# Spreading the branch gates over the RWKV pairs, wider chain loads, and block-diagonal RWKV scores in a hybrid attention / RWKV-7 / PEER layer

## The chip, the cores and the metric

One core of a Trainium2 chip runs the whole layer as one program. The metric is device time in microseconds of that core, as a median of runs. Besides TensorE (PE; its weight loads are PEld), VectorE (DVE), ScalarE (ACT), GpSimd (POOL) and SyncE (SP), the core has 16 DMA engines. DMAs are issued from in-order queues, here those of SP, ACT and POOL.

## The reference

One layer of a diffusion backbone on 512 latent tokens with a prefix of 256 context tokens, model width 1024, all in fp32.

```python
zx = split(modulate(rmsnorm(x, norm1_g), mod_x[0], mod_x[1]) @ w_in, IN_SPLIT_IDX)   # and zc of the context
o_ax = diff_post(diff_attention(qx, k_all, v_all, lam), ...)        # 8 heads, 512 queries on 768 keys
_, y_x = wkv_scan(s_ctx, scan_x)                                    # RWKV-7, 16 heads of 64, two directions
o_bx = rwkv_post(from_scan(y_x), ...)
g_a, g_b = split(sigmoid(zx[4]), 2)                                 # branch gates: 2 x 1024 columns of w_in
x = x + mod_x[2] * ((g_a * (o_ax @ w_branch_a) + g_b * (o_bx @ w_branch_b)) @ w_out)
x = x + mod_x[5] * peer_ffn(modulate(rmsnorm(x, norm2_g), ...), ...)  # top 16 of 16384 experts, 8 heads

def step(s, inp):                                                   # one token of the RWKV scan
    w, kk, a, k, v, r = inp
    sa = einsum('dbhij,dbhj->dbhi', s, kk)
    s = s * w[..., None, :] - sa[..., :, None] * (kk * a)[..., None, :] + v[..., :, None] * k[..., None, :]
    return s, einsum('dbhij,dbhj->dbhi', s, r)
```

## The kernel before

A framework puts the instructions of each engine into one fixed order: it simulates the program, takes the earliest instruction of the program text that its simulation finds ready, and fills gaps with later ones. So what stands later in the text can run earlier, across the stages below. Tiles come from pools with a fixed number of buffers, and an instruction waits until its buffer is free.

A product of full precision is three passes (`mm3`): weights and activations are split into a high part (ACT, line 95, `w_hi`) and a low part (DVE, line 96, `w_lo`). One column tile of 128 with 512 tokens is 24 matmuls of 512 columns.

The stages in order of time:

- **Set-up** (to about 65 us): modulation, norm, `hidden`, which also writes the modulated hidden state to the scratch tensor `hD`.
- **RWKV pairs** (`rw_pairs`, about 65 to 545 us): eight pairs of heads. Pair p projects k, r and v of pair p+1 (`rw_proj`, `shifted`; PSUM pool `pps` of 4 banks), makes the decayed operands `At` and `kb` of both directions (`rw_operands`), the bonus and transposed values (`rw_values`), and the chunk scores (`rw_scores`). The scores are 64x64 matmuls: per group of 8 chunks and per direction 16 of them into one `pq` tile of two banks (pool of 2 tiles), head 0 on rows 0 to 63, head 1 on rows 64 to 127. ACT copies `tt` and `kt` out, DVE masks `bt`, and SP stores them to the DRAM tensors `readD`, `scoreD`, `KBD`, `tD`, in runs of 1 KB for the first three. `rw_inverse` inverts 128 32x32 triangles at a time on DVE, in pairs 2, 3, 4, 6, 7 and after the last. Pair 7, which has no next projection, runs the first 5 (`NG`) of 16 gate tiles instead (`filler`).
- **Attention projections** (about 545 to 765 us): q, k, v of four head pairs.
- **Chain** (`rwkv_chain`, about 765 to 1112 us): 24 chunks of 32 tokens, one after the other, in two groups g: `reads` (line 659), `solve` (669), `state` (681, 687), `outputs` (700), `collect`. `load(c + 1)` fetches a chunk: per head side `cb` from `readD` and `scoreD` (64 partitions each) and `KBt` in runs of 512 bytes, `sv` and `XTz`; 14 DMAs on SP's queue, into 2 buffers (3 for `sv`). Attention (`attention`) fills the gaps: the first 25 of its 32 (head, query block) combines use PSUM pool `psO`; the last 7 use `psR`, a pool opened after the chain's PSUM is free. Heads 1 to 7 load `qr`, `kr`, `va` on POOL's queue (`att_load`).
- **Attention's end and gates** (about 1112 to 1206 us): `rwkv_centre`, the 7 last combines, `attention_norm`, and `gates`: the hidden state is read back from `hD`, split again, and gate tiles 5 to 15 are projected.
- **Merge** (`merge`, about 1206 to 1345 us), and **PEER** (to the end): `peer_route`, `peer_gates`, and `block_acts` for blocks of 128 experts, whose PSUM tile `ps_a` has 2 banks (`pa`) that ACT's gelu (line 1121) frees.

Of the kernel before, what the change touches and what calls it, by code (L numbers as in the profile page):

```python
# [9 lines left out]
F32 = mybir.dt.float32  # L10
# [11 lines left out]
S = 512  # L22
# [8 lines left out]
class K:  # L31
# [68 lines left out]
    def consts(self):  # L100
# [25 lines left out]
        self.hD = dt("hD", [KT, 128, S])  # L126
# [16 lines left out]
    def consts_late(self):  # L143
# [11 lines left out]
        self.ka1 = cp.tile([128, 8], F32, name="ka1")  # L155
        nc.vector.tensor_scalar(self.ka_, self.ka_, 0.5, None, op0=OP.mult)
        nc.vector.tensor_scalar(self.ka1, self.ka_, -1.0, 1.0, op0=OP.mult, op1=OP.add)
# [62 lines left out]
    def hidden(self, xt, n, i, hi, lo, pool):  # L220

        nc = self.nc
        for kt in range(KT):
# [4 lines left out]
            if i == 0:  # L228
                nc.sync.dma_start(self.hD[kt], h)
# [95 lines left out]
    NG = 5  # L325

    def gate(self, n, hx, gp, pp, tag):
# [6 lines left out]
        g = gp.tile([128, S], F32, name="st_r", bufs=2)  # L334
        nc.scalar.activation(g, px, AF.Tanh, scale=0.5)
        nc.sync.dma_start(self.gateD[n], g)

    def gates(self, gp, pp):
        nc = self.nc
        self.wn = 128  # L340
        hx = [gp.tile([128, KT, S], F32R, name=f"gh{i}") for i in range(2)]
        for kt in range(KT):
            raw = gp.tile([128, S], F32, name="gr", bufs=2)
            nc.sync.dma_start(raw, self.hD[kt])
            nc.scalar.copy(hx[0][:, kt], raw)
            nc.vector.tensor_tensor(hx[1][:, kt], raw, hx[0][:, kt].bitcast(F32), op=OP.subtract)
        for n in range(self.NG, 16):
            self.gate(n, hx, gp, pp, "ps_gt")
# [6 lines left out]
    def rwkv_open(self, es):  # L355
# [10 lines left out]
        self.At = self.Ai[:, :3072].rearrange("p (c a d x) -> p c a d x", c=12, a=2, d=2)  # L366
        for j in range(2):
            h = slice(64 * j, 64 * j + 64)
            nc.vector.tensor_copy(self.Ai[h, 3072:], self.ident[h, h])
# [78 lines left out]
    def rw_proj(self, p, mids=()):  # L448
# [11 lines left out]
        for o in (0, H):  # L460
            ps = self.ps.tile([128, 512], F32, name="pp")
            nc.tensor.matmul(ps[:, :H], self.bones, kk[:, o:o + H], start=True, stop=True)
            rs = self.rsqrt(self.stage1, ps[:, :H], H, 1.0, 1e-12, tag="kk")
            nc.vector.scalar_tensor_tensor(kk[:, o:o + H], k[:, o:o + H], self.kk_[:, p:p + 1], rs,
# [3 lines left out]
    def rw_operands(self, p, sg, k, kk, r):  # L468
# [5 lines left out]
        for dr in range(2):  # L474
# [5 lines left out]
            nc.vector.tensor_scalar(w, w, 1.0, None, op0=OP.add)  # L480
            nc.vector.tensor_tensor_scan(L, self.smask, w, 0.0, op0=OP.mult, op1=OP.add)
# [5 lines left out]
            for tk, cs in parts:  # L487
                nc.vector.scalar_tensor_tensor(kb[:, cs, 32:64], ch(a)[:, cs], 1.0, ch(fl(kk[:, tk])),
                                               op0=OP.add, op1=OP.mult)
# [4 lines left out]

            kr = (lambda x: x[:, :, ::-1]) if dr else (lambda x: x)
            for tk, cs in parts:
                nc.vector.tensor_tensor(kr(kb[:, cs, 0:32]), ch(fl(k[:, tk])), ch(a)[:, cs], op=OP.mult)
            wc = ch(w)
            if dr == 0:
                k2 = kb.rearrange("p c (i t) -> p c i t", i=2)  # L500
                nc.vector.tensor_tensor(k2, k2, wc[:, :, None, :].to_broadcast([128, 24, 2, 32]), op=OP.mult)
            else:
                nc.vector.tensor_tensor(kb[:, :, 0:32], kb[:, :, 0:32], kr(wc), op=OP.mult)
                nc.vector.tensor_tensor(kb[:, :, 32:64], kb[:, :, 32:64], wc, op=OP.mult)
            KB.append(kb)
        for j in range(2):
            nc.sync.dma_start(self.readD[:, j, :, p].rearrange("c r a d x -> r c (a d x)"),
                              self.At[64 * j:64 * j + 64].rearrange("p c a d x -> p c (a d x)"))
# [84 lines left out]
    def rw_pairs(self, filler):  # L593
# [3 lines left out]
        for p in range(8):  # L597
# [7 lines left out]
            if p in (2, 3, 4, 6, 7):  # L605
                self.rw_inverse((2, 3, 4, 6, 7).index(p))
# [851 lines left out]
```

## Time and profile before

| | |
|---|---|
| median of 3 runs | 2692.36 us (2684.4 to 2698.49) |
| profiled execution | 2696.16 us, span 2693.7 us |
| PE busy | 2448.3 us (91% of the span) |
| PE weight loads | 2097.4 us (78%) |
| DVE busy | 1973.3 us (73%) |
| ACT busy | 1180.8 us (44%) |
| POOL busy | 384.9 us (14%) |
| chain that ended last | PE 62%, DVE 15%, DMA 12%, ACT 5%, issue 4% |

Busy shares are means over stages with different limits, and matmuls overlap: their shown duration is longer than the interval at which they follow each other.

### The profile page before, as it was taken

To read this page: it belongs to the slowest core of one execution; us is meant where nothing else is said; L and a number is where in the kernel's file an instruction comes from. 1 tells how busy PE (TensorE), PEld (TensorE's weight loads), DVE (VectorE), ACT (ScalarE), POOL (GpSimd) and SP (SyncE) were. 2 spreads that over 40 slices of the span, in tenths; PEclk is the share of its full clock that TensorE was granted. 3 is DMA by queue.
4 is the path that set the end of the run, shared out by engine and by line. 5 is a ranking of instruction groups with operands and counts; after the bars stand their busy time and mean duration, and the time that the engine had idled before them with its cause. 6 is when DMAs were issued, how large, how long until landed. Compare 5 with 4: busy or idle time off the path is not lost.

```text
span 2693.7 us, 47831 instructions
## 1 busy us (share of the span) xinstructions
PE 2448.3 (91%) x18877; PEld 2097.4 (78%) x18877; DVE 1973.3 (73%) x3661; ACT 1180.8 (44%) x2173; POOL 384.9 (14%) x322
## 2 busy tenths in 40 slices
PE   6888777799979878999989988999999999989898
PEld 3776666688968767787768887998889999867677
DVE  5778987773547556748469998886587888878894
ACT  4676555433346555645243343554233333323232
POOL 0000000000110000000000000003344444444440
PEclk8999988799989999999989999999999999999999
DMA  6376666767579877544432443678999999999993
GB/s 256 99 158 153 152 136 155 196 200 244 143 171 204 165 154 151 129 133 133 160 125 95 140 150 129 257 264 337 331 336 329 339 327 336 337 356 366 380 336 109
DMA packets 344912, 584.04 MB, mean 217 GB/s; under 512 B 85552, under 2 KB 238768, under 8 KB 337904
## 3 DMA queue, kind: packets, MB, share of 16 engines
q1 hardware_dynamic: 293744, 400.74, 50.7%
q0 software_dynamic: 39664, 146.16, 15.5%
q10 hardware_dynamic: 11280, 34.08, 3.8%
q8 instruction: 148, 2.42, 0.4%
q14 instruction: 76, 0.62, 0.1%
HBM read 473.03 MB, written 107.48 MB: 216 GB/s over the span
## 4 chain that ended last, share of the span: by engine, by line
PE 62%; DVE 15%; DMA 12%; ACT 5%; issue 4%; SPq 2%; POOL 0%; ACTq 0%; DVEq 0%; POOLq 0%
PE ps_v L1149 6%; PE ps_v L1151 6%; PE ps_v L1148 6%; PE ps_a L78 5%; PE ps_a L79 5%; PE ps_a L80 5%; PE pp L78 4%; PE pp L79 4%; PE pp L80 4%; DMA cb<-scoreD 3%; PE ps_br L80 2%; PE ps_br L79 2%; PE ps_br L78 2%; PE ps_s L681 1%; PE ps_o L814 1%
## 5 line engine op out<-in xcount | busy, mean ns | idle before, releaser
L78 PE MATMUL ps_a<-h,u_hi 128*128 128x384 f32 x1024 | 349.1, 341 | 19.7 <-ACT act L1121 17.7
L80 PE MATMUL ps_a<-h,u_lo 128*128 128x384 f32 x1024 | 348.7, 341 | 5.9 <-DVE u_lo L72 5.9
L79 PE MATMUL ps_a<-h,u_hi 128*128 128x384 f32 x1024 | 346.8, 339 | 0.0
L69 ACT CAST u_hi<-u_raw 128x1024 fp32r<-128x1024 f32 x128 | 134.4, 1051 | 305.3 <-PE ps_a L79 284.4
L1086 POOL DMA_INDIRECT gr<-in_peer_u,ei x128 | 164.0, 1281 | 705.7 <-PE ps_a L79 483.1
L72 DVE TENSOR_TENSOR u_lo<-u_raw,u_hi 128x1024 fp32r<-128x1024 f32 x128 | 156.1, 1220 | 111.8 <-ACT u_hi L69 110.4
L78 PEld LDWEIGHTS ps_a<-h,u_hi 128*128 128x128 f32 x1024 | 195.1, 190 | 25.6 <-ACT act L1121 21.0
L1086 POOL DMA_INDIRECT gr<-in_peer_v,ei x128 | 179.9, 1406 | 202.4 <-DVE ra L1104 182.8
L80 PEld LDWEIGHTS ps_a<-h,u_lo 128*128 128x128 f32 x1024 | 194.5, 190 | 9.1 <-DVE u_lo L72 8.1
L79 PEld LDWEIGHTS ps_a<-h,u_hi 128*128 128x128 f32 x1024 | 194.9, 190 | 2.3
L96 DVE TENSOR_TENSOR w_lo<-w_raw,w_hi 128x1024 fp32r<-128x1024 f32 (+1 forms) x93 | 124.9, 1343 | 86.9 <-ACT w_hi L95 83.4
L1093 DVE CUSTOM_DVE_ANT_0 gr<-gr,ht 128x1024 f32<-128x1024 f32 x128 | 153.8, 1219 | 13.9 <-DMA gr<-in_peer_u,ei 13.8
L1104 DVE SCALAR_TENSOR_TENSOR ra<-gr,wk,ra 128x1024 f32<-128x1024 f32 x127 | 162.7, 1281 | 1.2 <-DMA gr<-in_peer_v,ei 0.2
L552 PE MATMUL pq<-At,kb 64*64 64x128 f32 x1536 | 115.6, 300 | 46.4 <-DVE bt L559 36.3
L1149 PE MATMUL ps_v<-v_lo,pw_hi 128*128 128x512 f32 x420 | 143.6, 402 | 11.4 <-DVE v_lo L1139 11.4
L552 PEld LDWEIGHTS pq<-At,kb 64*64 64x64 f32 x1536 | 98.1, 149 | 71.1 <-issue 59.6
L95 ACT CAST w_hi<-w_raw 128x1024 fp32r<-128x1024 f32 (+1 forms) x93 | 106.9, 1149 | 97.9 <-PE ps_br L79 52.1
L1148 PE MATMUL ps_v<-v_hi,pw_hi 128*128 128x512 f32 x420 | 126.3, 398 | 13.0 <-ACT v_hi L1138 13.0
L1151 PE MATMUL ps_v<-v_hi,pw_lo 128*128 128x512 f32 x420 | 133.7, 400 | 0.0
L69 ACT CAST pw_hi<-actl 128x384 fp32r<-128x384 f32 x72 | 37.0, 514 | 217.1 <-PE ps_v L1149 217.1
L1148 PE MATMUL ps_v<-w_hi,pw_hi 128*128 128x512 f32 x348 | 128.4, 401 | 4.0 <-issue 4.0
L1149 PE MATMUL ps_v<-w_lo,pw_hi 128*128 128x512 f32 x348 | 131.9, 398 | 0.0
(377 smaller groups left out, 6373.4 us busy)
## 6 DMA issues: line engine op xcount, KB each, us to landing
u_raw<-in_uT SPq DMA_DIRECT2D x128, 512.0 KB, 4.7
v_raw<-in_peer_v SPq DMA_DIRECT2D x70, 512.0 KB, 8.0
w_raw<-in_peer_v SPq DMA_DIRECT2D x58, 512.0 KB, 6.5
wm<-in_w_mod SPq DMA_DIRECT2D x24, 1024.0 KB, 7.8
gD<-gstage SPq DMA_DIRECT2D x12, 2048.0 KB, 9.3
gg<-gD SPq DMA_DIRECT2D x16, 1536.0 KB, 11.9
actD<-act SPq DMA_DIRECT2D x18, 768.0 KB, 3.8
actl<-actD SPq DMA_DIRECT2D x9, 1536.0 KB, 11.7
```

Of the source, the lines that this page charges most:

```text
L69: nc.scalar.copy(hi, raw)
L72: (lo_eng or nc.vector).tensor_tensor(lo, raw, hi.bitcast(F32), op=OP.subtract)
L78: mm(ps, lh[0], rh[0], start=first, stop=False)
L79: mm(ps, lh[0], rh[1], start=False, stop=False)
L80: mm(ps, lh[1], rh[0], start=False, stop=last)
L552: nc.tensor.matmul(ps[i][h, c, :], KB[dr][h, g, :], at, start=True, stop=True)
L1086: nc.gpsimd.indirect_dma_start(out=r, out_offset=None, in_=self.A[name], in_offset=bass.IndirectOffsetOnAxis(ap=self.ei[:, k:k + 1], axis=0))
L1093: nc.vector.tensor_tensor_reduce(out=r, in0=r, in1=self.ht, scale=1.0, scalar=0.0, op0=OP.mult, op1=OP.add, accum_out=w[:, k:k + 1])
L1104: nc.vector.scalar_tensor_tensor(self.ra, r, w[:, k:k + 1], self.ra, op0=OP.mult, op1=OP.add)
L1148: mm(pc[t][d], w[0][:, ts], v[0][:, c[d]], start=first, stop=False)
L1149: mm(pc[t][d], w[0][:, ts], v[1][:, c[d]], start=False, stop=False)
L1151: mm(pc[t][d], w[1][:, ts], v[0][:, c[d]], start=False, stop=last)
```

## The change

Gate tiles 2p and 2p+1 are now computed inside RWKV pair p from the hidden state in SBUF; `gates`, `hD` and the filler are gone. The scores use block-diagonal 128x128 operands `kz` (both heads in one matmul, zeros elsewhere); the multiplication by the decay `w`, which was three wide DVE instructions on `kb`, now writes `kz` in 36 small ones per pair. One PSUM pool of 7 banks serves the whole front part. Scores and operands go to `cbD` and `KBD`, laid out by chunk and row: stored in runs of 512 bytes, read with one 4 KB run per partition, `cb` over 128 partitions. `sv` and `XTz` loads of the chain go to POOL's queue. The normalisation of kk starts on ACT and has one DVE instruction less per half; `a + 1` is an instruction of its own. In PEER's first phase `block_acts` alternates between two pools of 2 banks.

```diff
@@ scratch tensors
-        self.readD = dt("readD", [12, 2, 64, 8, 2, 2, 64])
-        self.scoreD = dt("scoreD", [12, 2, 64, 8, 2, 2, 64])
-        self.KBD = dt("KBD", [12, 2, 64, 8, 2, 2, 64])
+        self.cbD = dt("cbD", [24, 256, 8, 2, 64])
+        self.KBD = dt("KBD", [24, 128, 8, 2, 64])
...
-            if i == 0:
-                nc.sync.dma_start(self.hD[kt], h)
...
@@ rw_proj
-            rs = self.rsqrt(self.stage1, ps[:, :H], H, 1.0, 1e-12, tag="kk")
+            nc.scalar.activation(y, ps[:, :H], AF.Abs_reciprocal_sqrt, bias=self.tiny)
+            nc.scalar.activation(q, y, AF.Square, scale=math.sqrt(0.5))
+            nc.vector.scalar_tensor_tensor(q, ps[:, :H], 1e-12, q, op0=OP.add, op1=OP.mult)
+            nc.vector.scalar_tensor_tensor(y, q, 1.5, y, op0=OP.subtract, op1=OP.mult)
...
@@ rw_operands
+            nc.vector.tensor_scalar(a, a, 1.0, None, op0=OP.add)
...
-            if dr == 0:
-                k2 = kb.rearrange("p c (i t) -> p c i t", i=2)
-                nc.vector.tensor_tensor(k2, k2, wc[:, :, None, :].to_broadcast([128, 24, 2, 32]), op=OP.mult)
-            else:
-                nc.vector.tensor_tensor(kb[:, :, 0:32], kb[:, :, 0:32], kr(wc), op=OP.mult)
-                nc.vector.tensor_tensor(kb[:, :, 32:64], kb[:, :, 32:64], wc, op=OP.mult)
...
@@ rw_scores
+            for i in range(2):
+                c4, g4 = slice(4 * i, 4 * i + 4), slice(cg * 8 + 4 * i, cg * 8 + 4 * i + 4)
+                for dr in range(2):
+                    kz = self.kz[i][dr]
+                    for j in range(2):
+                        h = slice(64 * j, 64 * j + 64)
...
+                        if dr == 0:
+                            eng.tensor_tensor(zo, zi, w[0][h, g4, None, :].to_broadcast([64, 4, 2, 32]), op=OP.mult)
+                        else:
+                            eng.tensor_tensor(zo[:, :, 0, ::-1], zi[:, :, 0], w[1][h, g4], op=OP.mult)
+                            eng.tensor_tensor(zo[:, :, 1], zi[:, :, 1], w[1][h, g4], op=OP.mult)
+                    ps = self.ps.tile([128, 512], F32, name="pp").rearrange("p (c x) -> p c x", c=4)
                     for c in range(4):
...
-                            nc.tensor.matmul(ps[i][h, c, :], KB[dr][h, g, :], at, start=True, stop=True)
+                        nc.tensor.matmul(ps[:, c, :], kz[:, c, :], at, start=True, stop=True)
...
+            for dst, src in ((self.cbD[:, 64:192], bt), (self.KBD, kt)):
+                nc.sync.dma_start(dst[cg * 8:cg * 8 + 8, :, p].rearrange("c r d x -> r c (d x)"),
+                                  src.rearrange("p c d x -> p c (d x)"))
...
@@ rw_pairs
-            nx = self.rw_proj(p + 1, [lambda: ups((1, 0), (1, 1)), lambda: ups()]) if p < 7 else filler([lambda: ups((1, 0), (1, 1)), lambda: ups()])
+            mids = [lambda: ups((1, 0), (1, 1))]
+            nx = self.rw_proj(p + 1, mids) if p < 7 else mids[0]()
+            gate(2 * p)
             KB = self.rw_operands(p, sg, *st[:3])
...
+            gate(2 * p + 1)
             self.rw_values(p, st[0], st[2], st[3])
-            self.rw_scores(p, KB)
+            self.rw_scores(p, KB, sg)
...
@@ rwkv_chain, load(c)
-                ld(cb[j][h], rows(self.readD))
-                ld(cb[j][r], rows(self.scoreD))
-                ld(KBt[j][c % NL][r], rows(self.KBD))
+                ld(cb[j], self.cbD[c, 128 * j:128 * j + 128])
+                ld(KBt[j][c % NL][64 - 64 * j:128 - 64 * j], self.KBD[c, 64 * j:64 * j + 64])
                 for d, t in enumerate((32 * c, 32 * ((7 if c < 8 else 31) - c))):
-                    nc.sync.dma_start(sv[j][i][64 - 64 * j:96 - 64 * j, d], self.vTD[t:t + 32, j])
+                    nc.gpsimd.dma_start(sv[j][i][64 - 64 * j:96 - 64 * j, d], self.vTD[t:t + 32, j])
             for q in range(4):
-                nc.sync.dma_start(XTz[c % NL][32 * q:32 * q + 32, q], self.xD[q // 2, c, q % 2])
+                nc.gpsimd.dma_start(XTz[c % NL][32 * q:32 * q + 32, q], self.xD[q // 2, c, q % 2])
...
@@ block_acts, peer
-        ps = self.pa.tile([128, S], F32, name="ps_a")[:, :ND]
+        ps = (pa or self.pa).tile([128, S], F32, name="ps_a")[:, :ND]
...
-                    self.block_acts(g * AB + b, act[:, b, :])
+                    self.block_acts(g * AB + b, act[:, b, :], pa1 if b % 2 else None)
...
@@ front
-        pps = self.pool("pps", 4, space=PSUM)
-        self.ps = pps.__enter__()
         mps = self.pool("mps", 1, space=PSUM)
         self.mps = mps.__enter__()
+        pps = self.pool("pps", 7, space=PSUM)
...
@@ mixers
-                self.gates(gp, pp)
```

## Rows read from the trace of the kernel before

**Rows 1.** Windows by stage: PE, PEld, DVE, ACT, POOL busy (instructions); clock, DMA share, GB/s.

```profile
65.00:545.00 480.00, 389.75 (x2845) 316.80 (x2845) 378.79 (x766) 275.68 (x580) 4.44 (x8) 0.91 0.64 151
545.00:765.00 220.00, 214.24 (x1806) 198.81 (x1804) 112.61 (x189) 74.02 (x132) 10.38 (x10) 0.99 0.59 183
765.00:1112.00 347.00, 295.70 (x6242) 251.66 (x6243) 222.14 (x489) 192.26 (x436) 22.57 (x37) 0.93 0.86 170
1112.00:1206.00 94.00, 91.53 (x474) 75.12 (x472) 51.87 (x102) 53.84 (x105) 0.00 (x0) 1.00 0.42 133
1206.00:1345.00 139.00, 139.00 (x565) 106.16 (x565) 85.21 (x119) 54.88 (x75) 0.00 (x0) 1.00 0.48 151
1345.00:1850.00 505.00, 471.17 (x3002) 438.06 (x3001) 434.41 (x1065) 221.20 (x417) 6.46 (x7) 0.97 0.50 172
```

**Rows 2.** Waits in 765 to 1112 us: who, for whom, us, times, longest.

```profile
POOL va L766 <- PE ps_o L814: 170.1, 6, 49.5
...
PE ps_r L659 <- DMA cb<-scoreD: 16.3, 11, 2.9
...
PE ps_u L669 <- ACT rhs L662: 12.5, 3, 5.0
...
PE ps_r L659 <- DMA XTz<-xD: 6.6, 3, 3.5
```

**Rows 3.** DMA in 765 to 1112 us: a queue's packets, MB, share; issues with landing time.

```profile
q1 hardware_dynamic: 79399, 46.03, 69.8%
...
cb<-scoreD SPq DMA_DIRECT2D x44, 256.0 KB, 7.1
...
cb<-readD SPq DMA_DIRECT2D x43, 256.0 KB, 6.6
...
w_raw<-in_w_g SPq DMA_DIRECT2D x2, 512.0 KB, 4.6
```

**Rows 4.** Groups in 1112 to 1206 us: busy, mean ns, idle before them.

```profile
L96 DVE TENSOR_TENSOR w_lo<-w_raw,w_hi 128x1024 fp32r<-128x1024 f32 x13 | 15.9, 1222 | 21.7 <-ACT w_hi L95 18.6 <-ACT pdT L811 2.4 <-PE ps_gt L80 0.7
```

**Rows 5.** DVE groups in 65 to 545 us.

```profile
L559 DVE TENSOR_TENSOR bt<-pq,mask 128x256 f32<-128x256 f32 x96 | 40.3, 419 | 27.3 <-ACT kt L558 27.2
...
L501 DVE TENSOR_TENSOR kb<-kb,sgw 128x1536 f32<-128x1536 f32 x8 | 14.0, 1749 | 0.0
...
L480 DVE TENSOR_SCALAR sgw<-sgw 128x768 f32<-128x768 f32 x16 | 8.9, 554 | 2.0 <-ACT sgw L443 2.0
L53 DVE TENSOR_SCALAR kk_v<-pp 128x384 f32<-128x384 f32 x16 | 8.9, 553 | 6.0 <-PE pp L462 6.0
...
L504 DVE TENSOR_TENSOR kb<-kb,sgw 128x768 f32<-128x768 f32 x8 | 7.6, 950 | 0.0
...
L432 DVE TENSOR_TENSOR lul<-bo,luh 64x256 fp32r<-64x256 f32 x16 | 6.7, 419 | 7.0 <-ACT luh L429 6.8
...
L584 DVE TENSOR_TENSOR X<-X,Xt 128x135 f32<-128x135 f32 x10 | 2.9, 293 | 0.2
```

**Rows 6.** Timeline of DVE: start, duration; neighbours that overlap.

```profile
216.55 0.69 DVE L492 TENSOR_TENSOR At<-P,st_r 128x512 f32<-128x512 f32 x1
217.15 0.42 DVE L582 TENSOR_TENSOR Xt<-Tm,X 128x252 f32<-128x252 f32 x1
```

**Rows 7.** Chain that ended last: start, us, unbroken runs of matmuls.

```profile
496.59 1.92 PE pq L552 x28
...
1142.41 1.34 PE ps_o L814 x12
```

**Rows 8.** Windows: one 60 us stretch of the pairs, columns as in rows 1.

```profile
240.00:300.00 60.00, 47.25 (x402) 37.68 (x398) 51.30 (x116) 37.78 (x83) 1.11 (x2) 1.00 0.75 165
```

**Rows 9.** DMA in 65 to 545 us: SP's queue.

```profile
q1 hardware_dynamic: 95551, 54.95, 52.7%
```

**Rows 10.** Waits of PE in 1393 to 1850 us.

```profile
PE ps_a L78 <- ACT act L1121: 17.7, 11, 2.8
```

**Rows 11.** POOL's DMA issues by line: ns min/median/max.

```profile
L757 POOL DMA_DIRECT2D kr<-kTD x14: 587/597/602, 784.1 to 1021.8; - x14
```

More of the change, by code (lines that the diff above doesn't have):

```diff
@@ L333, in gate @@
             self.mm3(px, (w[0][:, kt], w[1][:, kt]), (hx[0][:, kt], hx[1][:, kt]), kt == 0, kt == KT - 1)
-        g = gp.tile([128, S], F32, name="st_r", bufs=2)
+        g = gp.tile([128, S], F32, name="st_g", bufs=1)
         nc.scalar.activation(g, px, AF.Tanh, scale=0.5)
         nc.sync.dma_start(self.gateD[n], g)
[L338 to L348, printed above, removed]
     def rwkv_open(self, es):
@@ L591, in rw_inverse, with rw_pairs @@
             o += n
-    def rw_pairs(self, filler):
+    def rw_pairs(self):
+        gate = lambda n: self.gate(n, self.hx, self.stage, self.ps, "pp")
         st = self.rw_proj(0)
@@ L1109, with block_acts @@
     AB = 4
-    def block_acts(self, n, out):
+    def block_acts(self, n, out, pa=None):
         nc = self.nc
@@ L1168, in peer @@
         with self.pool("rt1", 1, side="right") as b1, self.pool("pg", 4, space=PSUM) as self.pg, \
-                self.pool("ap", 2, side="left") as ap:
+                self.pool("ap", 2, side="left") as ap, self.pool("pa1", 2, space=PSUM) as pa1:
             self.row_tokens()
@@ L1287, in front @@
             self.hidden(ct, CT, 1, self.hc[0], self.hc[1], hp)
-        mps.__exit__(None, None, None)
-        with wps, self.pool("pqs", 2, space=PSUM) as self.pq, self.pool("stg", 2, side="right") as self.stage, self.pool("stg1", 1, side="right") as self.stage1:
+        with wps, self.pool("stg", 2, side="right") as self.stage, self.pool("stg1", 1, side="right") as self.stage1:
             inv = self.pool("inv", 1, side="left")
@@ L1296, in front @@
                 self.rw_lora(w0)
-                self.rw_pairs(lambda mids: [(f(), self.gate(n, self.hx, self.stage, self.ps, "pp"))
-                                            for n, f in enumerate(mids + [lambda: None] * (self.NG - 2))])
+                self.rw_pairs()
             inv.__exit__(None, None, None)
-        pps.__exit__(None, None, None)
-        mps = self.pool("mps", 1, space=PSUM)
-        self.mps = mps.__enter__()
-        pps = self.pool("pps", 7, space=PSUM)
-        self.ps = pps.__enter__()
         self.wn = 256
@@ L1348, in mixers @@
             self.wpool = self.wps.enter_context(self.pool("wp", 2, side="left"))
-            with self.pool("gt", 1, side="left") as gp, self.pool("rpp", 2, space=PSUM) as pp, \
+            with self.pool("rpp", 2, space=PSUM) as pp, \
                     self.pool("atr", 3, space=PSUM) as psR:
```

62 lines of the change are left out of this document (28 added, 34 removed).

## Prediction

> **What bounds the kernel now.** I read the windows by stage first. In the RWKV pairs (65 to 545 us) no engine is full: PE 389.75 and DVE 378.79 of 480 us, 81% and 79%, at a granted clock of 0.91. The attention projections are PE's (214 of 220). In the chain (347 us) PE is busy for 295.70 at 0.93, and the DMA engines for 0.86 of the time. The stretch behind the chain is PE's alone (91.53 of 94), and so is the merge (139 of 139): its 24 column tiles cost 139 / 24 = 5.8 us each [rows 1]. So work that moves from the stretch behind the chain into the pairs moves from a full PE to one with 90 us idle.
>
> The waits of the chain come next: PE stands 16.3 us for `cb<-scoreD` and 6.6 for `XTz`, and 12.5 at the start for ACT's `rhs`, which is queued there behind casts that await their own loads [rows 2]. The DMA view says why: SP's queue alone moves 46 MB in 79,399 packets, about 580 bytes each, and takes 69.8% of the engines' time; a half `cb` of 256 KB lands after 7.1 or 6.6 us, a whole weight tile of 512 KB after 4.6 [rows 3].
>
> **The change part by part.**
>
> *Gates leave the stretch behind the chain.* Eleven tiles of 5.8 us are 64 us of PE. What is left there: PE 91.5 - 64 = 27.5; on DVE 51.9 less eleven `w_lo` of 1.222 (13.4), 38 at most [rows 1, 4]. Left are the 7 last combines, which by their pool cannot start before the chain ends, and the norm. If they overlapped perfectly the stretch would be 38 us (-56). If the dependent steps of a combine kept their pace, it would shrink only a little; I set the weak end at -15. No engine is full there any more, but one combine is a line of PE, DVE, ACT, PE steps; I take 51 us, **-43**.
>
> *Gates enter the pairs: PE.* +64 us.
>
> *Scores, PE.* Before: 1536 instructions (each fp32 matmul shows as two); an unbroken run is 28 in 1.92 us, 69 ns each, 105 us. After: 384 whole-array matmuls, 768 instructions. The nearest are the 128x128 ones with 128 columns of attention: 12 in 1.34 us, 112 ns each, 86 us [rows 7]. So -19 us, and PE in the pairs comes to 390 + 64 - 19 = 435.
>
> The Trainium skill (TensorEngine Tiling (Array Packing), Theoretical Speedup) speaks against this part: a contraction of 64 or fewer rows gains up to 2x from splitting the array, and block-diagonal operands give that back. By that rule the scores would cost PE as much as before, and the sum would be 19 us of PE higher. The rows side with the change here, since the split instructions follow each other at 69 ns and not at half of 112.
>
> *Scores, DVE.* Per pair 12 instructions of 64x256 (419 ns, L432) and 24 of 64x128 (nearest 128x135, 293 ns, L584): 5.0 + 7.0 = 12.0 us. Away go one of 1749 (L501) and two of 950: 3.65. Net +8.4 by durations [rows 5]; neighbours on DVE overlap by some 0.09 us (216.55 + 0.69 against 217.15) [rows 6], and 33 instructions more give back 3.0: +5.4. I take +6 a pair, +48 (43 to 67). The eleven gates bring 11 x 1.2 = 13 of `w_lo`. The kk normalisation loses two of 553 ns (L53), `a + 1` adds two of 554 (as L480): nothing. DVE comes to 379 + 61 = 440.
>
> *The pairs' span.* At today's density, 440 / 0.79 = 557, **+77**, the upper end. At the density of the busiest stretch, 51.30 of 60 us [rows 8], 515, +35. The lower end is +0: the projections show PE 97% full where no dependence is in the way [rows 1]. I take 507, **+27**: the gates depend on nothing but weights; 27.3 us of DVE's idle time is spent inside the scores waiting for ACT to empty a `pq` bank [rows 5], and there DVE now has the next `kz` to write and PE seven banks; and pair 7 sheds three gates. What the change makes late: `w` must live until the last `kz` of its direction is written, so ACT's tanh for the next pair waits for that, with the `tt` and `kt` copies and a gate's cast behind it on ACT, and the scan behind it on DVE. The next projection's shifts, the gates and the inverses cover it; without cover it is part of the +77.
>
> *Queues and DMA in the pairs.* SP loses six stores a pair and gets two gate weights and two gate stores. 36,864 runs of 1 KB become 73,728 of 512 bytes. A packet on this queue takes 0.527 x 480 x 16 / 95,551 = 42 ns [rows 9]; if the halves cost as much as the wholes, that is 98 us of all 16 engines, if only bytes count, nothing. With 8.6 MB of gates (37 us at 151 GB/s for a share of 0.64) the engines have at most 0.64 x 480 + 98 + 37 = 442 busy in 507 us, so stores grow slower but nothing is bound. Zero, under cover of DVE and PE.
>
> *Chain.* The 22.9 us of waits for `cb` and `XTz` go when loads land like a weight tile. Of the 12.5 at the start half is loads: -6. Stalled PE runs at the lower clock; from 0.93 to 0.97 on 296 us is some 10 us. **-40**. Ends: PE's 296 us at full clock are 275, and 95% full that is 290 us, -57; if the recurrence read, solve, state takes over as the limit, -5. SP issues 4 instead of 14 DMAs a chunk, POOL 8 of 0.6 us [rows 11], 4.8 us of a chunk's 14.5 (347 / 24).
>
> *PEER's first phase.* PE waits 17.7 us in all for the gelu that frees `ps_a` [rows 10]. Two banks more remove between nothing (DVE has 434 of 505 [rows 1]) and all; I take **-8**.
>
> *One PSUM pool* over the boundary of pairs and projections: 0 to -6, the idle PE time of the projections; **-2**.
>
> Sum: 27 - 40 - 43 - 8 - 2 = -66. The profiled execution, 2696.2 us (span 2693.7 and 2.5 around it), becomes 2630; the median of the runs lies 3.8 lower, at 2692.4, so I forecast **2626 us**.
>
> **The rivals.**
>
> *The pairs stretch at their old density* (+77). For it: DVE and PE become nearly equal loads of 440 and 435, tied by short steps, and `w` lives longer. Against it: part of the idle time has its cause removed. It gives 2692 - 16 = 2676. To reach no gain the pairs would need +93.
>
> *The chain is not faster* (-5 in place of -40). For it: PE idles 347 - 296 = 51 us there, and only 22.9 of these end with a chain load [rows 1, 2]; the rest is the recurrence. Against it: a late load also lets the clock fall, and delays what stands behind it on PE. It gives 2661.
>
> *POOL's queue holds the chain back*: the slower one. `sv` and `XTz` now stand in one queue with attention's loads, and POOL waited for a combine to free `va` 6 times for 170.1 us, 28 each [rows 2]. A load is asked for one chunk ahead, 14.5 us. If each such wait stood ahead of the next chunk's loads, 28 - 14.5 = 14 us would be lost 6 times, 84 us; with the chain's saving of 40 gone too the sum is +58: 2750. It decides from 11 us lost per wait. Against it: PE's order is fixed, so what frees `va` and what frees `XTz` come in the order for which the queue was laid out.
>
> The Trainium skill (SBUF — State Buffer, SBUF: two separate sides) adds that descriptors for POOL's DMAs are written by GpSimd, which a copy on DVE in a two-port mode locks out. The trace shows no such stretching: POOL's issues of `kr` take 587 to 602 ns while DVE is 64% busy [rows 1, 11]. By that rule, with one copy of 0.55 us (as L53) ahead of each issue, 8 issues would take 9 us of a chunk, still under 14.5.
>
> **How the numbers follow.** Forecast 0.68; pairs at old density 0.16; chain not faster 0.08; POOL's queue 0.08. Low end: pairs +0, chain -57, stretch behind it -52, PEER -12: -121, 2571. High end: pairs +77 with the rest as taken, 2676; with the POOL case and half of the tail of the pairs case outside. Range 2571 to 2676. About 0.5% (13.5 us, below 2679) is what a measurement tells from no change. The pairs case, at 2676, splits around that bound: 0.08 faster, 0.05 same, 0.03 slower; POOL's into 0.03 same and 0.05 slower. Faster: 0.68 + 0.08 + 0.08 = 0.84; same 0.08; slower 0.08.
>
> **What would show it.** Pairs: last scores some 27 us later than before, DVE near 87% full up to there; 77 later is the first rival. Chain: no wait of PE on `cb`, DMA share near a half, clock over 0.95, about 305 us long. If PE still waits there for `XTz` or `sv`, it is the POOL queue. Behind the chain: about 50 us to the first `ps_br`, with no `ps_gt` of gates. PEER: the wait of `ps_a` on the gelu under 10 us. The sum is most in danger from the pairs' density and from the combines behind the chain, should these keep their old pace.

## The result, and the profile after

The changed kernel takes 2590.66 us (median of 4 runs, 2584.66 to 2592.65), the kernel before 2692.91 in the runs beside it: ratio 0.9606, 95% interval 0.9588 to 0.9623. The forecast was 2626, within 2571 to 2676: faster by 35 us than its likeliest value. The profiled execution has a span of 2590.1 us (before 2693.7).

Five marks in the trace divide the span of every kernel below: the last score matmul, the first read of the chain (`ps_r`), the start of its last transpose of an output, the first `ps_br`, and the end. In us of the profiled executions:

| | last score | first read | last transpose | first ps_br | end | pairs / projections / chain / behind it / rest |
|---|---|---|---|---|---|---|
| before | 538.7 | 762.1 | 1112.0 | 1207.3 | 2693.7 | 538.7 / 223.4 / 349.9 / 95.3 / 1486.4 |
| after | 520.6 | 742.5 | 1058.2 | 1112.8 | 2590.1 | 520.6 / 221.9 / 315.7 / 54.6 / 1477.3 |
| difference | | | | | -103.6 | -18.1 / -1.5 / -34.2 / -40.7 / -9.1 |
| forecast | | | | | -66 | +27 / -2 / -40 / -43 / -8 |

Four of the five stages came out within 6 us (one execution each; how far such marks repeat stands under the experiments). The pairs did not: forecast 27 us longer, they are 18 shorter. The windows of these stages, of the kernel after (columns as in rows 1):

```profile
65.00:521.00 456.00, 416.79 (x2335) 358.28 (x2336) 405.15 (x909) 299.96 (x599) 2.21 (x4) 0.97 0.64 164
521.00:742.00 221.00, 213.81 (x1752) 198.35 (x1750) 155.35 (x323) 76.50 (x145) 20.75 (x30) 0.99 0.66 207
742.00:1058.00 316.00, 285.95 (x6304) 242.32 (x6305) 222.02 (x489) 191.80 (x435) 109.18 (x213) 0.97 0.70 189
1058.00:1113.00 55.00, 42.99 (x219) 31.33 (x217) 37.58 (x88) 35.34 (x83) 0.00 (x0) 0.84 0.17 56
1248.00:1750.00 502.00, 475.55 (x3056) 439.31 (x3055) 438.98 (x1073) 228.22 (x427) 9.77 (x10) 0.98 0.52 179
```

Beside [rows 1]: in the pairs the clock rose from 0.91 to 0.97, and DVE and PE went from 79% and 81% busy to 89% and 91%. In the projections DVE has 43 us more than before. The chain's DMA share fell from 0.86 to 0.70, its clock rose from 0.93 to 0.97. Behind the chain DVE lost 14 us, as counted, and PE 48.5 where 64 were counted, at a clock of 0.84 in place of 1.00.

The groups of instructions in the pairs, kernel after (busy, mean ns, idle before them), which answer to [rows 5] and [rows 7]:

```profile
L546 PE MATMUL pp<-At,kz 128*128 128x128 f32 x768 | 106.2, 295 | 35.7 <-DVE kz L539 15.4 <-DVE kz L535 7.3 <-ACT luh L419 5.2
L535 DVE TENSOR_TENSOR kz<-kb,sgw 64x256 f32<-64x256 f32 x96 | 40.0, 417 | 1.9 <-PE pp L546 0.6
L551 DVE TENSOR_TENSOR bt<-pp,mask 128x256 f32<-128x256 f32 x92 | 36.9, 419 | 3.6 <-ACT kt L550 2.2
L574 DVE TENSOR_TENSOR Xt<-Tm,X 128x87 f32<-128x87 f32 (+15 forms) x91 | 30.8, 338 | 6.2 <-POOL X L570 5.0 <-DMA Tm<-tD 0.2
L576 DVE TENSOR_TENSOR X<-X,Xt 128x87 f32<-128x87 f32 (+15 forms) x91 | 30.7, 337 | 0.9
L538 DVE TENSOR_TENSOR kz<-kb,sgw 64x128 f32<-64x128 f32 x96 | 27.2, 283 | 1.3
```

The wait of `bt` for ACT's `kt`, 27.2 us before, is 2.2. PE had waited longest for `bt` before:

```profile
PE pq L552 <- DVE bt L559: 36.3, 22, 4.2
```

In place of that wait PE now waits for `kz`, 25 us with L538. The `kz` instructions cost what the rows of before said (419 and 293 ns forecast, 417 and 283 found). And half of the inverses' steps (`X`, `Xt`) are gone from the pairs: 91 of 186 stand there, before 154; the rest fills gaps in the projections. That is the 43 us of DVE above.

The waits of the chain after, 742 to 1058 us, for [rows 2]:

```profile
POOL va L760 <- PE ps_o L808: 26.7, 5, 16.5
...
PE ps_u L663 <- ACT rhs L656: 12.6, 4, 4.9
...
PE ps_r L653 <- DMA cb<-cbD: 7.1, 6, 2.6
```

PE's wait for `cb` went from 16.3 to 7.1 us and that for `XTz` is gone; the one for `rhs` at the start, 12.5, stayed at 12.6, of which the forecast had counted 6 as saved. POOL's waits for `va` shrank from 170.1 to 26.7 us. The DMA view of the same stretch, for [rows 3]:

```profile
q1 hardware_dynamic: 12750, 38.27, 42.4%
q0 software_dynamic: 8432, 20.59, 26.7%
...
cb<-cbD SPq DMA_DIRECT2D x44, 512.0 KB, 6.3
...
sv<-vTD POOLq DMA_DIRECT2D x88, 64.0 KB, 5.8
...
XTz<-xD POOLq DMA_DIRECT2D x88, 32.0 KB, 2.8
```

SP's queue moves 3 KB a packet in place of 580 bytes: a sixth of the packets for five sixths of the bytes. A whole `cb` lands in 6.3 us, where each half took 6.6 or 7.1.

### The profile page after: what moved, and what is told of

The parts are those of the page before. It is cut to its first block, busy times and chain, and to the rows that moved or that the text cites. A ratio compares the mean times of both kernels' runs of the same rounds, so it can differ in the third digit from the quotient of the medians.

```text
span 2590.1 us, 46535 instructions
## 1 busy us (share of the span) xinstructions
PE 2411.5 (93%) x18109; PEld 2078.5 (80%) x18109; DVE 2025.8 (78%) x3919; ACT 1184.6 (46%) x2171; POOL 482.8 (19%) x518
## 4 chain that ended last, share of the span: by engine, by line
PE 62%; DVE 20%; DMA 9%; ACT 4%; issue 4%; SPq 0%; POOL 0%; ACTq 0%; DVEq 0%; POOLq 0%
PE ps_v L1143 6%; PE ps_v L1145 6%; PE ps_v L1142 6%; PE ps_a L80 5%; PE ps_a L78 5%; PE ps_a L79 5%; PE pp L79 3%; PE pp L80 3%; PE pp L78 3%; PE ps_s L675 2%; PE ps_br L79 2%; PE ps_br L80 2%; PE ps_br L78 2%; DMA cb<-cbD 2%; PE ps_o L808 2%
## 5 line engine op out<-in xcount | busy, mean ns | idle before, releaser
L546 PE MATMUL pp<-At,kz 128*128 128x128 f32 x768 | 106.2, 295 | 35.7 <-DVE kz L539 15.4
L78 PE MATMUL pp<-hx,w_hi 128*128 128x512 f32 x336 | 134.9, 402 | 3.4 <-ACT sgw L433 2.4
L80 PE MATMUL pp<-hx,w_lo 128*128 128x512 f32 x336 | 134.1, 399 | 2.0 <-DVE w_lo L96 2.0
L79 PE MATMUL pp<-hx,w_hi 128*128 128x512 f32 x336 | 133.0, 396 | 1.8 <-DVE hx L231 1.8
L546 PEld LDWEIGHTS pp<-At,kz 128*128 128x128 f32 x768 | 98.4, 207 | 42.9 <-ACT kt L550 18.5
```

Source lines behind the costliest of these rows:

```text
L78: mm(ps, lh[0], rh[0], start=first, stop=False)
L79: mm(ps, lh[0], rh[1], start=False, stop=False)
L80: mm(ps, lh[1], rh[0], start=False, stop=last)
L546: nc.tensor.matmul(ps[:, c, :], kz[:, c, :], at, start=True, stop=True)
```

## The experiments

Three theories of the pairs, formed after the result. **A**: DVE sets their length, and they shrank since 43 us of inverses slid out. **B**: the gates fill PE's gaps and keep its clock up. **C**: the new scores took a wait away that ran through PE, ACT and DVE. For the chain, **P** says the packets of the operands were its cost, **Q** says SP's queue was. Other letters, and the B of e6 and e10 (a line of dependent steps), are explained in the expectations. The marks of all runs (the total is a median; the stages are those of the one profiled execution, which in e5 took 2607.0 us):

| | total us, ratio [interval] | pairs | projections | chain | behind | rest |
|---|---|---|---|---|---|---|
| after | 2590.66, 0.9606 [0.9588, 0.9623] | 520.6 | 221.9 | 315.7 | 54.6 | 1477.3 |
| e1 | 2620.67, 0.9721 [0.9696, 0.9746] | 477.9 | 259.2 | 308.2 | 98.9 | 1473.6 |
| e2 | 2632.49, 0.9758 [0.9732, 0.9784] | 564.5 | 220.6 | 320.3 | 57.1 | 1469.1 |
| e3 | 2590.14, 0.9614 [0.9582, 0.9646] | 518.3 | 224.4 | 319.0 | 51.2 | 1473.8 |
| e4 | 2588.97, 0.9596 [0.9561, 0.9632] | 519.0 | 224.7 | 317.7 | 52.3 | 1472.4 |
| e5 | 2596.65, 0.9617 [0.9589, 0.9646] | 525.1 | 223.0 | 327.6 | 58.6 | 1470.6 |
| e6 | 2563.68, 0.9498 [0.9470, 0.9526] | 491.5 | 229.1 | 314.8 | 52.4 | 1479.6 |
| e7 | 2624.72, 0.9725 [0.9696, 0.9754] | 519.1 | 227.6 | 357.4 | 52.8 | 1466.4 |
| e8 | 2596.14, 0.9624 [0.9596, 0.9651] | 520.3 | 222.5 | 321.0 | 55.6 | 1468.8 |
| e9 | 2587.74, 0.9598 [0.9566, 0.9630] | 521.5 | 225.7 | 310.5 | 51.3 | 1475.9 |
| e10 | 2581.28, 0.9571 [0.9540, 0.9602] | 508.8 | 226.5 | 319.5 | 55.5 | 1467.9 |
| e11 | 2595.59, 0.9624 [0.9597, 0.9651] | 520.1 | 222.9 | 319.3 | 50.9 | 1480.6 |
| e12 | 2591.88, 0.9618 [0.9590, 0.9647] | 526.3 | 227.9 | 314.9 | 55.2 | 1465.7 |

A stage that no edit touches shows how far the marks of one execution can be trusted: the chain, whose code is the same in every row but e7 and e8, lies between 308 and 328 us, the rest between 1466 and 1480 (e11, which edits it, left out). So a few us in the chain or in the rest say nothing. The pairs repeat better: 518 to 521 in the six kernels that do the same there (after, e3, e4, e7, e8, e11).

**e1: the gates back behind the chain.** All else as changed.

```diff
-            gate(2 * p)
...
-            gate(2 * p + 1)
...
+            nx = self.rw_proj(p + 1, [...]) if p < 7 else filler([...])
...
+                self.gates(gp, pp)
```

> The changed kernel with one part undone: gate tiles 5 to 15 run behind the chain again, from the hidden state read back (the first 5 fill pair 7, as before). Theory A (DVE bounds the pairs, and they became short because 43 us of inverses slid behind them): the eleven gates bring DVE only 13 us, so without them the pairs' last score comes 5 to 15 us earlier than 521 us, the stretch behind the chain grows back by 40 us to about 95, total 2615 to 2625. Rival B (the gates themselves made the pairs short, by filling PE's waits and holding its clock at 0.97): the pairs get longer without them, last score at 535 or later, clock there about 0.92, total 2640 or more.

2620.67, as A had it for the total; the last score is not where A had it: it comes 43 us earlier, where A had 5 to 15. Windows of pairs and projections of this kernel:

```profile
65.00:478.00 413.00, 359.96 (x2067) 305.19 (x2065) 374.32 (x837) 268.28 (x568) 1.11 (x2) 0.98 0.63 158
478.00:737.00 259.00, 227.68 (x1802) 207.24 (x1801) 191.27 (x422) 92.36 (x166) 27.21 (x40) 0.93 0.65 201
```

Without the gates the pairs are 43 us shorter, and the clock is 0.98 all the same, which speaks against B. DVE is 91% busy, and two thirds of the inverses now run in the projections, which grow by 37 us and fall to a clock of 0.93. So what the gates cost the front is read at the chain's first read, 742.5 against 737.1: 5 us for some 57 of PE (416.8 - 360.0). They give back 44 behind the chain. So the projections do not take every amount of inverses for nothing: 124 of the 186 steps run there, 95 in the changed kernel, and in e1 the store of the last inverse (711.5 us, 9.0 long) stands in the chain that ended last, ahead of the first read.

**e2: the old scores** (64x64 operands, long multiplications, `pq` tiles of two banks, four banks for the rest).

```diff
-                    ps = self.ps.tile([128, 512], F32, name="pp").rearrange(...)
...
-                        nc.tensor.matmul(ps[:, c, :], kz[:, c, :], at, ...)
...
+                pq = self.pq.tile([128, 2, 4, 128], F32, name="pq")
...
+                            nc.tensor.matmul(ps[i][h, c, :], KB[dr][h, g, :], at, ...)
```

> The changed kernel with the scores as before: 64x64 matmuls into tiles of two banks (pool of 2), the decay multiplied by three wide DVE instructions, PSUM pool of 4 banks for the rest. Gates, layout and loads stay changed. Theory A: DVE is relieved of 48 us in the pairs, so they end at the same time or up to 20 us earlier, or inverses slide back into them; total 2575 to 2600. Rival C (seven banks and one-bank score tiles made the pairs short by taking away the 36 us that PE and the 27 us that DVE waited): the pairs' last score comes 20 to 45 us later than 521, total 2610 to 2640.

2632.49, as C had it. The pairs are 44 us longer than in the changed kernel, and 26 longer than before: gates with the old scores cost about what I had forecast for the whole change. The pairs' window and two waits of this kernel:

```profile
65.00:565.00 500.00, 438.84 (x3100) 362.82 (x3098) 390.11 (x755) 293.92 (x597) 4.45 (x8) 0.94 0.63 160
```
```profile
PE pq L542 <- DVE bt L549: 36.7, 20, 10.3
...
DVE bt L549 <- ACT kt L548: 31.3, 39, 1.5
```

DVE is back at 78% and both waits of before are there. The new scores cost DVE more and yet win 44 us; e5 and e9 ask with which of their parts.

**e3 and e4: the inverses moved in the text**, ahead of a pair's operands, or all six behind the pairs.

```diff
-            if p in (2, 3, 4, 6, 7):
-                self.rw_inverse((2, 3, 4, 6, 7).index(p))
...
-        self.rw_inverse(5)
+        for b in range(6):
+            self.rw_inverse(b)
```

> The changed kernel with the five inverses called at the top of their pair, ahead of everything else of that pair, so that the program order puts them inside the pairs. Theory A: 43 us of DVE work come back into the pairs, which then end 30 to 45 us later than 521; the projections get no shorter, total 2615 to 2635. Rivals B and C: DVE has room, the pairs end less than 10 us later, total 2590 to 2600.

> The changed kernel with all six inverses called after the pairs. Theory A: DVE loses another 61 us in the pairs, whose last score comes 25 to 55 us earlier than 521; DVE is then near full in the projections (155 + 61 of 224 us), and the chain may start late by the inverses that are not done; total 2555 to 2600. Rivals B and C: the pairs end at 515 or later, total 2590 to 2610.

Neither moved anything on the chip: the steps of the inverses run over the same stretch as in the changed kernel (first and last start 209 to 699 us in e3, 212 to 701 after), with the same number of them in the pairs to a few. The framework fills gaps with them wherever they stand in the text. For A both runs are void; e6 takes their place.

**e5: one-bank tiles, but four banks of their own.**

```diff
-                    ps = self.ps.tile([128, 512], F32, name="pp").rearrange(...)
+                    ps = self.pq.tile([128, 512], F32, name="pq").rearrange(...)
...
-        pps = self.pool("pps", 7, space=PSUM)
+        pps = self.pool("pps", 4, space=PSUM)
...
+        with wps, self.pool("pqs", 4, space=PSUM) as self.pq, ...
```

> The changed kernel, its scores still block-diagonal and in one-bank tiles, but these tiles come from a pool of four banks of their own, and projections, gates and operands have four others, as before the change. It tells the banks apart from the rest of what the old scores undid at 44 us (last score 520.6 us with the change, 564.4 with the old scores). Theory C1, the score tiles are one bank each and evicted one at a time, so that PE and DVE run ahead of ACT whatever pool they come from: last score 515 to 527, total 2585 to 2600. Theory C2, the seven shared banks let the gates and projections run ahead of the scores: last score at 540 or later, total 2610 or more.

C1: last score 525.1, total 2596.65. With as many banks as the old scores had, in the same split, 39 of the 44 us are there. PE's waits in the pairs of this kernel:

```profile
PE pp L431 <- ACT luh L419: 14.8, 5, 6.3
PE pq L546 <- DVE bt L551: 10.7, 24, 1.9
```

An old `pq` tile covers two banks and comes free only after the last of eight evictions (six by ACT, two by DVE); of the new ones each comes free after four. As many stops, 24 against 20, but 0.4 us each in place of 1.8. With fewer banks for the projections PE waits 14.8 us for ACT's LoRA operand, 5.2 in the changed kernel; all in all the seven shared banks add some 4.5 us (525.1 - 520.6), little more than the 518 to 521 by which the same pairs differ.

**e6: 1 of 31 steps of the inverses.**

```diff
-        for s in range(31):
+        for s in range(1):
```

> The changed kernel with 1 of the 31 steps of the block inverses; the other 30 steps, some 59 us of DVE in the pairs and 62 in the attention projections, are left out, so its output means nothing. Theory A, DVE (89% busy) sets the length of the pairs: 35 to 59 us of the 59 come back, the last score stands at 462 to 486 us in place of 520.6. Theory B, the pairs are a line of short steps between PE, ACT and DVE, in whose gaps the inverses lie: the last score stands at 505 or later, and DVE's density falls to 80% or less. In both the projections, where PE is 96% full, stay at 218 to 224 us. Total by A 2530 to 2560, by B 2575 to 2592.

Last score 491.5, between the two theories. Windows of pairs and projections of this kernel:

```profile
65.00:492.00 427.00, 409.94 (x2335) 351.52 (x2335) 359.57 (x736) 292.55 (x593) 5.60 (x10) 0.99 0.70 177
492.00:721.00 229.00, 215.01 (x1770) 199.43 (x1772) 98.03 (x135) 76.75 (x144) 17.31 (x24) 0.98 0.61 196
```

46 us less of DVE made the pairs 29 shorter, and then PE is 96% busy at a clock of 0.99: it is the next bound, at not much under 427 us. A holds in kind, at 0.6 us for one of DVE: PE's waits for `kz` fell from 25 us to 4.6. In the projections 57 us less of DVE brought nothing (229 us, where 218 to 224 were expected): in these amounts the steps lie in PE's shadow there.

**e9: the old operands in the new tiles.**

```diff
...
-                        at = self.Ai[:, o:o + 64]
...
-                        nc.tensor.matmul(ps[:, c, :], kz[:, c, :], at, ...)
+                        for j in range(2):
+                            h = slice(64 * j, 64 * j + 64)
+                            at = self.Ai[h, o:o + 64]
...
+                            nc.tensor.matmul(ps[h, c, :], KB[dr][h, g, :], at, ...)
```

> The changed kernel with the score matmuls of before (64x64 operands, two to a chunk, no block-diagonal kz and none of its 36 DVE instructions a pair; the three long multiplications of a pair are back), but in the change's tiles of one bank from the seven shared banks, each emptied as soon as its eight small matmuls are done. Nobody's version so far: the old scores (last score 564.4 us) and the changed ones (520.6) differ in the operands and in the tile. Theory D, the tile of one bank does it and the block-diagonal operands only cost DVE its 48 us: last score 480 to 505, DVE busy for some 360 us up to there, total 2550 to 2580. Theory E, the block-diagonal operands do it, since PE takes half as many instructions and starts on a tile after three short multiplications instead of a long one over all 24 chunks: last score 540 or later, total 2610 or more. Between 505 and 540 both have a share.

Last score 521.5, total 2587.74 (0.9598 against 0.9606): the same as with block-diagonal operands. So what the new scores bring comes from the tile of one bank, with the some 4.5 us of the seven shared banks (e5); on balance the operands bring nothing. Windows of the pairs, and the scores' group:

```profile
65.00:522.00 457.00, 418.77 (x3094) 351.13 (x3092) 366.32 (x708) 293.77 (x590) 3.33 (x6) 0.96 0.66 168
```
```profile
L540 PE MATMUL pp<-At,kb 64*64 64x128 f32 x1536 | 95.2, 281 | 17.4 <-DVE bt L545 7.9 <-ACT st_g L334 5.4 <-DVE kb L491 2.2
```

The split form takes 95.2 us of PE and the block-diagonal one 106.2: 11 us more, where I had counted 19 saved. Not all of the 11 belongs to the operands: in e6 the same block-diagonal matmuls take 97.2. The rule of the Trainium skill (TensorEngine Tiling (Array Packing), Theoretical Speedup) that packing gains up to 2x for contractions of 64 rows or fewer has the sign right here, with a gain of 1.02 to 1.12.

The rest was not expected: DVE has 39 us less in the pairs, and they are no shorter. Theory D had asked for 480 to 505. The 39 are a difference: the operands take some 60 us less (89.6 of `kz` away, 29 of long multiplications back), and 22 us of inverses came back into the pairs, 124 steps in place of 91 (window of one of the two instructions of a step):

```profile
65.00:522.00 457.00, 41.81 (x124) 0.96 0.66 168
```

Whether they hold the pairs back there was not tried: the split operands without the inverses were not run.

**e12: `bt` read out of a bank ahead of ACT's copies**, in the kernel of e9.

```diff
+                    nc.vector.tensor_tensor(bt[:, c4, dr], ps[:, :, 0:64], ...)
                     for j in range(2):
                         nc.scalar.copy(tt[q, c4, dr], ps[q, :, 0:32])
                     nc.scalar.copy(kt[:, c4, dr], ps[:, :, 64:128])
-                    nc.vector.tensor_tensor(bt[:, c4, dr], ps[:, :, 0:64], ...)
```

> The one-bank split scores (last score 521.5 us, DVE 366 us of 457 in the pairs, 80%, against 405 with the block-diagonal operands) with one line moved: DVE's bt is read out of a score bank ahead of ACT's three copies, not behind them. Open is why 39 us less of DVE made the pairs no shorter. Theory F, DVE's queue stands at its head for ACT's copies from the same bank (27.2 us of waits of bt for kt, 34 times) and PE then stands 22 us for bt; with the kz multiplications these gaps had something to do. Then bt first takes most of the waits away, ACT has the slack for them (294 us of 457), last score 495 to 512, total 2560 to 2580. Rival G, PE with 419 us busy and its rows of the gates and projections is the bound there, and ACT's copies only come later: last score 516 or later, total 2583 or more.

F falls: 526.3, total 2591.88. PE's waits in the pairs:

```profile
PE pp L540 <- ACT kt L546: 9.6, 6, 6.3
PE pp L428 <- ACT kt L546: 9.6, 17, 2.1
```

In e9 PE stood 14.5 and 7.9 us at these places for `bt`; now it stands 9.6 and 9.6 for `kt`. The wait is for whoever empties a bank last, and its name changed more than its length (22.4 to 19.2 us). The marks of G came, but they do not show that PE is the bound.

**e10: 48 of the 288 `kz` multiplications on GpSimd**, in the changed kernel.

```diff
-                        eng = nc.vector
+                        eng = nc.gpsimd if dr == 0 and j == 1 else nc.vector
```

> The changed kernel with 48 of the 288 kz multiplications (64x256, those of one direction and one half; 20 us of DVE) on GpSimd instead. Theory A, DVE sets the length of the pairs: with 59 us of inverses left out the last score came 29 us earlier, so 20 us bring 8 to 14, last score 505 to 513, total 2576 to 2586. Theory B, a matter of dependent steps: GpSimd needs more than the 417 ns of DVE for one, and PE waits for it: last score at 521 or later, total 2592 or more.

As A had it: last score 508.8, total 2581.28, ratio 0.9571, the lowest of the kernels that do all the work; its four runs (2580.62 to 2581.79) lie below the four of the changed kernel, though the intervals of the two ratios overlap. The `kz` instructions of e10 (ns min/median/max):

```profile
L539 DVE TENSOR_TENSOR kz<-kb,sgw x96: 273/284/848, 115.8 to 507.5; 64x128 f32<-64x128 f32 x96
L538 DVE TENSOR_TENSOR kz<-kb,sgw x96: 270/289/867, 119.3 to 507.3; 64x128 f32<-64x128 f32 x96
L535 POOL TENSOR_TENSOR kz<-kb,sgw x48: 722/778/2347, 108.1 to 504.2; 64x256 f32<-64x256 f32 x48
L535 DVE TENSOR_TENSOR kz<-kb,sgw x48: 404/408/952, 111.8 to 506.1; 64x256 f32<-64x256 f32 x48
```

One takes 778 ns on GpSimd and 408 on DVE, and still it pays, since PE waited 0.7 us in all for it and its weight loads 7. Some of DVE's own `kz` are stretched to 848 to 952 ns, where without GpSimd none was above 425. The Trainium skill (SBUF — State Buffer, SBUF: two separate sides) says that a DVE instruction with two inputs in SBUF and a GpSimd one that reads SBUF shut each other out for a whole instruction; the stretched maxima agree with that, and the medians, which hardly moved, show that most instructions are not hit. In sum it counts all the same:

```profile
65.00:509.00 444.00, 410.81 (x2329) 352.50 (x2328) 395.54 (x862) 294.28 (x593) 46.39 (x52) 0.98 0.65 167
```

47 instructions and 20 us left DVE in the pairs, and its busy time fell by 10 (405.15 to 395.54); the others grew by the rest, the remaining `kz` and the steps of the inverses most.

**e7: the old layout of the chain's operands**, `sv` and `XTz` left on POOL.

```diff
...
-                ld(cb[j], self.cbD[c, 128 * j:128 * j + 128])
+                ld(cb[j][h], rows(self.readD))
+                ld(cb[j][r], rows(self.scoreD))
```

> The changed kernel with the chain's operands stored and loaded as before (half tiles over 64 partitions, six loads a chunk on the SP queue), while the loads of values and inverses stay on the POOL queue. Theory P, the number of packets is what the change bought in the chain: PE waits 12 us or more for cb in the chain, the chain lasts 330 us or more in place of 313, total 2610 or more. Theory Q, it is SP's queue, which the move of eight loads a chunk to POOL has relieved: PE's waits for cb stay under 8 us, the chain under 320 us, total 2600 or less. The stores of the pairs go back to the old form too; where the last score moves by more than 5 us, the stretch in front of the chain is read by itself.

P: the chain lasts 357.4 us, total 2624.72, and the pairs stay at 519.1 with the old stores. Window of the chain, and PE's longest wait in it:

```profile
747.00:1104.00 357.00, 304.08 (x6307) 257.67 (x6306) 223.97 (x493) 194.59 (x440) 108.93 (x213) 0.91 0.79 167
```
```profile
PE ps_r L657 <- DMA cb<-scoreD: 26.7, 15, 5.4
```

26.7 us of waits for `cb` in place of 7.1, and the clock at 0.91 in place of 0.97, make PE's busy time 18 us longer for the same instructions: 20 + 18 = 38 of the 42 us. e7 brings small packets, half tiles over 64 partitions and six issues a chunk back together, and does not tell them apart. The number of issues is not it, as e8 shows with 12. For the packets speaks that the same bytes on SP's queue (38 MB) take 52.4% of the engines' time in 72,378 packets and 42.4% in 12,750, and that loads which the edit does not touch land later too: `XTz`, on POOL's queue, after 4.6 us in place of 2.8.

**e8: `sv` and `XTz` back on SP's queue.**

```diff
-                    nc.gpsimd.dma_start(sv[j][i][...], self.vTD[t:t + 32, j])
+                    nc.sync.dma_start(sv[j][i][...], self.vTD[t:t + 32, j])
```

and `XTz` likewise.

> The changed kernel with the eight loads a chunk of values and inverses back on the SP queue (12 issues a chunk there), operands loaded over 128 partitions as in the change. Theory P (packets): the queue is short of nothing, chain 309 to 317 us, total within 5 us of 2591. Theory Q (queue): the waits of PE for the inverses come back at 5 us or more, chain 320 us or more, total 2598 or more. By the rival of my prediction that POOL's queue holds the chain back it would even be faster: chain under 309 us.

The chain is at 321.0, a little over the marks of P and at the edge of those of Q, but inside what it shows where nothing is changed in it, and the total 2596.14 has an interval that overlaps the changed kernel's. PE waits 8.2 us for `cb`, and none for `XTz`, the sign by which Q was to be known. With large packets the queue of the small loads is worth nothing that this can measure; Q falls as far as these marks reach, and so does the rival of the prediction in which POOL's queue holds the chain back.

**e11: one pool for `ps_a`** in PEER's first phase.

```diff
-                    self.block_acts(g * AB + b, act[:, b, :], pa1 if b % 2 else None)
+                    self.block_acts(g * AB + b, act[:, b, :])
```

> The changed kernel without the second pool of two banks for ps_a in PEER's first phase, everything else as changed. Forecast's term: the wait for the gelu comes back with 10 to 18 us, from the first ps_br to the end 5 to 10 us longer than the 1477 of the changed kernel, total 2596 to 2603. Rival, DVE and the loads would have taken that time anyway: total within 3 us of 2592.

Inconclusive in the total. PE's waits from 1300 to 1750 us, first in e11, then in the changed kernel:

```profile
PE ps_a L78 <- ACT act L1115: 17.7, 11, 2.8
PE ps_a L80 <- DVE u_lo L72: 2.9, 3, 2.0
```
```profile
PE ps_a L78 <- ACT u_hi L69: 8.5, 12, 1.0
PE ps_a L80 <- DVE u_lo L72: 5.5, 5, 2.0
```

The wait for the gelu is back with the 17.7 us of [rows 10]. With the pool it goes, and a wait for the casts of the next operand, 8.5 + 5.5, stands there instead: 6.6 us are won, against 8 forecast. The stage's length (1480.6 against 1477.3, and 1466 to 1480 elsewhere) cannot tell 6.6 us from nothing.

## Why the prediction was right, and which step failed

Undone one at a time, the parts cost 0.0115 (gates), 0.0152 (scores) and 0.0119 (layout) of 2693 us: 31, 41 and 32, and 5 or less for the pool of `ps_a`. That is 104 to 109, where the whole change brought 106 by its ratio: the parts hardly lean on each other, and no further cause is needed. Each part is known to some 8 us and the sum less well, so a small further cause is not shut out; the kk normalisation and `a + 1` had no run of their own.

*Gates leave the stretch behind the chain*: forecast -43, found -40.7. The combines kept some of their pace: 55 us for 43 of PE at a clock of 0.84. That 51 came near is partly luck: PE's remainder was counted at 27.5, and 51 was chosen between the two ends, not worked out.

*Chain*: forecast -40, found -34.2. The mechanism was right in kind; of the waits 9.2 for `cb` and 6.6 for `XTz` went, none of the 6 for `rhs`, and the clock (0.93 to 0.97) took 10 off PE's busy time. These are 26 of the 34; the other 8 lie inside the scatter of the chain. A whole `cb` does not land like a weight tile (6.3 us, not 4.6), and the DMA share is 0.70, not near a half. In the rival of POOL's queue the bound of 11 us a wait is 66 / 6, with the chain's saving kept; with the saving gone, as that rival has it, 26 / 6 = 4 us would decide.

*PEER and the PSUM boundary*: 6.6 of waits for 8, 1.5 for 2; that the last stage is 9.1 shorter confirms neither, since that stage scatters by 14. *Stores in runs of 512 bytes*: nothing forecast, and in e7 the pairs are no shorter (519.1) with the old ones.

*The pairs' span* is the step that failed: 507 us forecast from 65 us on, 456 found. Its terms:

- *DVE comes to 440* failed: 405 found in the pairs. The work was sized well, since another 43 us of inverses moved on (405 + 43 = 448). What I did not see is that these steps need not stay: they are fill, and the projections held 43 us more of them at no cost, as e6 shows by taking them away there without effect (in e1, with 84 us of them there, they did cost). At the density of the forecast, 405 in place of 440 is 40 of the 51 us; by the 0.6 of e6, 43 us of DVE are 27 of span.
- *PE comes to 435* added busy time at the old clock. The 390 us at 0.91 are 362 at 0.98, and e1, with the new scores and without the eleven gates, has 360.0 at 0.98; the gates add 57 (416.8 - 360.0), where 64 were counted. I gave the clock back to PE in the chain and left it out in the pairs.
- *The density* was to rise from 79% to 87% and came to 89%, so this term was near. It was a wait: e5 and e9 show that a score tile over two banks held it down, and that a tile of one bank is worth 39 us (e5), 43 with the seven shared banks (e9). The wait of `bt` for `kt` was named, and the banks too, and I gave them 50 us (557 to 507).

The block-diagonal operands, for which the change is named, bring nothing on balance: -19 us of PE were forecast and -9 found beside the old kernel (115.6 to 106.2), of which the clock alone (0.91 to 0.97) makes 7, and the split form in the same tiles takes 11 less still. The rival of the old density is what e2 shows for the change without its tiles: 390 us of DVE in 500, 78%.

Open is what holds the pairs of e9 and e12 at 457 to 461 us with DVE at 80% and PE at 92%. It is not DVE's time alone (39 us less brought nothing), though inverses took part of what came free, and not the order in which a bank is emptied. In the changed kernel DVE's time does count: 46 us less gave 29 (e6), 10 less gave 12 (e10). A version with the split operands that also turns its free DVE time into a shorter span was not found.

## What to carry to other kernels

Where two engines at 80% hand tiles to each other, look first at how much one tile holds and how many evictions free it: splitting a PSUM tile into banks that come free one by one was worth 40 us here, while the costlier operands beside it were worth nothing on balance. Ask of each instruction in a full stage whether it must be there or only fills a gap; what fills can move on. And when a stall goes, scale the busy time of PE to the clock that it will then have.

## What the runs showed that was not expected

ACT and DVE empty a score bank one after the other. Timeline of the changed kernel, ACT's last copy and DVE's `bt` of one bank (start, duration):

```profile
246.25 0.37 ACT L550 COPY kt<-pp 128x256 f32<-128x256 f32 x1
```
```profile
246.65 0.42 DVE L551 TENSOR_TENSOR bt<-pp,mask 128x256 f32<-128x256 f32 x1 [0.86 <-ACT kt L550]
```

`bt` starts as `kt` ends, after 0.86 us of waiting, though both only read and read different columns. In none of the 96 banks does `bt` start sooner than 0.03 us after its `kt`; with the lines exchanged (e12) ACT waits for DVE instead. It is a wait for a semaphore of the program; no run lets the two read one bank at once. In this program a bank costs the sum of its readers' times.

A block-diagonal score matmul takes 138 ns an instruction (106.2 us / 768) and not the 112 that runs of 12 had shown. The 112 was right for the distance of two starts, which is the median here too. Two things come on top: 37 of the 50 unbroken runs are one tile, 8 instructions, and the last one of a run counts with its whole 275 ns (8 take 1.13 us at 248.12 us), and three stretches of scores ran at the lower of the two clocks (0.50 of full, 1.2 GHz), where they follow each other after 213 ns (window of the middle one, PE and PEld of this line alone):

```profile
418.00:423.00 5.00, 5.00 (x26) 5.00 (x25) 0.50 1.07 269
```

In these stretches the granted clock went with PE's stops, up and down: 0.97 to 0.91 in the chain when e7 put 20 us of waits back, 0.99 to 0.93 in the projections when e1 filled them with inverses and PE was busy for 88% of them in place of 97%.
